# A two-layer RG-LRU / GLA trunk on one core: another opening, GLA values of two heads side by side, three gate projections after the recurrences

## The chip, the core and the metric

The kernel runs on one core of a Trainium2 chip. The core has five engines with queues of their own: TensorE (PE in the profile, with its weight loads as PEld), VectorE (DVE), ScalarE (ACT), GpSimd (POOL) and SyncE (SP), which here issues every DMA. The metric is device time in microseconds of one execution; lower is better. The kernel before was timed three times: 1184.10, 1184.95 and 1185.15 us, median 1184.95 us.

## What is computed

512 positions of 1024 features pass through two layers. Each layer is a token mixer and then a gated ConvFFN, and each of these four sublayers has an RMS norm with adaLN scale and shift ahead and an RMS norm with an adaLN gate behind it. All of it is float32.

```python
def reference(x, c, ...):                       # x (1, 512, 1024), c (1, 1024)
    c_act = jax.nn.silu(c)
    for i in range(2):
        mod = (c_act @ ada_w[i] + ada_b[i])[:, None, :]
        sh_m, sc_m, gt_m, sh_f, sc_f, gt_f = jnp.split(mod, 6, axis=-1)
        h = rmsnorm(x, norm_g[i, 0]) * (1.0 + sc_m) + sh_m
        y = rglru_mixer(h, ...) if i == 0 else gla_mixer(h, ...)
        x = x + gt_m * rmsnorm(y, norm_g[i, 1])
        h = rmsnorm(x, norm_g[i, 2]) * (1.0 + sc_f) + sh_f
        x = x + gt_f * rmsnorm(conv_ffn(h, ...), norm_g[i, 3])
    return x

def rglru_mixer(h, w_in, conv_w, conv_b, wa, ba, wx, bx, lam, w_out):
    gate_br, x_br = jnp.split(h @ w_in, 2, axis=-1)
    x_br = causal_dwconv(x_br, conv_w, conv_b)             # 4 taps
    r   = sigmoid(block_diagonal(x_br, wa) + ba)           # 4 blocks of 256
    i_g = sigmoid(block_diagonal(x_br, wx) + bx)
    a = exp(-8 * r * softplus(-lam)); u = sqrt(1 - a * a) * i_g * x_br
    hs = scan(h_t = a_t * h_{t-1} + u_t)
    return (gelu(gate_br) * hs) @ w_out

def gla_mixer(h, ...):          # q, k: 4 heads of 128; v, r: 4 heads of 256; chunked scan
    q, k, v, r, z = split(h @ w_in); log_alpha = log_sigmoid(z @ w_alpha + b_alpha) / 16
    o = gated_linear_attention(q, k, v, log_alpha)
    return (rmsnorm(o) * silu(r)) @ w_out
```

## The kernel before

Everything is kept transposed: a feature tile is 128 features on the partitions by 512 positions in the columns, so x, h and each product are 8 such tiles. TensorE's products are split: a weight tile is loaded in float32 into a `raw` buffer, ScalarE makes its rounded part (CAST, `w<-raw`), VectorE the rest (TENSOR_TENSOR, `w<-raw,w`), and `mm3` makes three fp32r matmuls of them: high part by high part of h, high by low, low by high. A few small products (`e.mms` on float32 tiles) run as float32 in two passes each, and the trace counts each pass.

The program is not emitted in the order in which it is written. `Sched` records every instruction with its operands and an estimated cost, and `order` makes a list schedule: each engine takes, among its instructions whose operands and buffers its own estimate calls ready, the one with the longest path to the end (TensorE and SyncE: the one that was written first). The engines then run these lists strictly in order, with semaphores between them. Buffers come from pools: 43 general tiles `g`, 8 split weight tiles `w`, 3 `raw`, 2 `araw`, 7 PSUM banks `mm` and one PSUM bank `nr` for the norms' sums.

The stages that the change touches:

- **Opening** (layer 0's first norm and the RG-LRU input products). x comes in 8 loads of 256 KB; ScalarE squares each tile, VectorE adds them up in one sum, `rstd_bcast` sums over the partitions by matmuls with a column of ones (`nr<-const,g`, 128x1), ScalarE scales, GpSimd raises to the power -1/2 (`pow`), VectorE multiplies the identity by the result (`dg`, four TENSOR_SCALAR), and a float32 matmul with ones spreads it over all partitions (`nr<-g,const`). For each input tile k there are then two adaLN columns (`ada_col`: a 512 KB load and one VectorE STT over 1024 columns with a sum, `w<-w,const`), one weight unit `rgx` with the columns of NX = 6 output tiles, and the tile's h: VectorE multiplies by the norm, ScalarE applies scale and shift and casts, VectorE subtracts. The 6 products stay open in 6 PSUM banks over all eight k; the last two (`rgx2`) follow, each in one piece.
- **RG-LRU.** `conv4` takes each input product out of PSUM (one ScalarE instruction, three VectorE STT). `gproj(m)` is a gate projection of 24 matmuls, `gates(b)` the two sigmoid products of block b: float32 on unsplit weights, or fp32r on split ones for the blocks in GFR = (1, 2). `recur` is the recurrence of four tiles, `gmul` the product that goes into `out_proj`. RGG says which gate projections stand ahead of which block: ((), (0,), (1,2,3,4), (5,6,7)), with `gates(3)` last.
- **GLA.** For each head: the diagonal (`diag_start`), the values (`vproj`, 96 matmuls of 256 columns, `mm<-w,g`), two r projections of 24 matmuls of 512 columns, seven levels of the triangle (`level_x` on VectorE and ScalarE, `level_mm`: four float32 matmuls of 64 columns, then a copy_predicated), the part between the chunks (`inter_x`, `inter_mm`), and `attend`.
- **Norms.** All 19 norms go through `rstd_from` with its multiplied identity.

## Time and profile before

| what | value |
|---|---|
| median of three runs | 1184.95 us |
| span of the profiled execution, first to last instruction | 1182.5 us |
| PE busy | 1158.9 us, 98% |
| PEld / DVE / ACT / POOL busy | 1017.0 / 867.3 / 553.6 / 24.4 us |
| first lasting stretch of products on PE | from 23.81 us |
| granted TensorE clock | 0.999 |
| DMA | 157.44 MB, mean 133 GB/s |

The profiled execution's own time is its span, 1182.5 us, 2.45 us under the median. Busy time is a union over an engine's instructions, and a matmul's end is modelled; so what a matmul costs in a stream is read here from the starts of the streams that follow each other, divided by the number of matmuls, and not from the mean duration of one.

### The profile page before, as it was taken

What the parts mean: (1) busy time and instruction counts of PE and PEld (TensorE: products, weight loads), DVE (VectorE), ACT (ScalarE), POOL (GpSimd) and SP (SyncE); (2) the same over time, 40 slices, a digit from 0 to 9 for tenths busy, and PEclk for the clock granted to TensorE, in tenths of its full rate; (3) what the DMA queues carried; (4) which work ended last, traced back from release to release, by engine and by line L of the source; (5) the groups of instructions that cost most, each with busy time, mean ns of one, the idle gap of its engine ahead of it and who ended that gap; (6) DMA issues with size and microseconds to landing.
All of it is one profiled execution on the core that took longest, in us unless ns stands there. A gap on an engine that the chain in (4) does not pass through costs nothing.

```text
span 1182.5 us, 16970 instructions
## 1 busy us (share of the span) xinstructions
PE 1158.9 (98%) x6664; PEld 1017.0 (86%) x6664; DVE 867.3 (73%) x1470; ACT 553.6 (47%) x874; POOL 24.4 (2%) x37
## 2 busy tenths in 40 slices
PE   4999999999999999999999999999999999999998
PEld 3878899988888888899999899999988888888897
DVE  7999999988988956558779767458845556645635
ACT  5688864743333324434478344254643333424421
POOL 1000001000000000000000000000000000000000
PEclk9999999999999999999999999999999999999999
DMA  8956562477787843232412211203243333332202
GB/s 338 312 170 202 200 214 73 160 249 252 249 260 223 261 126 93 88 90 59 144 55 90 72 54 55 72 27 118 72 125 97 100 91 105 90 107 90 72 1 72
DMA packets 45857, 157.44 MB, mean 133 GB/s; under 512 B 4977, under 2 KB 7281, under 8 KB 45778
## 3 DMA queue, kind: packets, MB, share of 16 engines
q1 hardware_dynamic: 45778, 156.36, 41.6%
q8 instruction: 52, 0.85, 0.3%
q14 instruction: 27, 0.22, 0.1%
HBM read 154.25 MB, written 2.10 MB: 132 GB/s over the span
## 4 chain that ended last, share of the span: by engine, by line
PE 90%; DVE 5%; ACT 3%; issue 1%; DMA 1%; SPq 0%; POOL 0%; DVEq 0%; POOLq 0%
PE mm L435 88%; ACT g L411 2%; PE nr L435 1%; DVE g L377 1%; DVE w L364 1%; ACT L411 1%; DVE g L364 1%; ACT w L416 1%; DVE gh L377 1%; DVE g L393 1%; DVE w L377 1%; DMA const<-in_xT_dram 0%; DMA raw<-in_wall_dram 0%; DVE araw L377 0%; SPq L441 0%
## 5 line engine op out<-in xcount | busy, mean ns | idle before, releaser
L435 PE MATMUL mm<-g,w 128*128 128x512 f32 (+1 forms) x5114 | 957.5, 348 | 5.6 <-ACT g L416 2.5
L435 PEld LDWEIGHTS mm<-g,w 128*128 128x128 f32 x5114 | 826.2, 189 | 130.4 <-ACT g L416 4.1
L364 DVE TENSOR_TENSOR w<-raw,w 128x1024 fp32r<-128x1024 f32 (+1 forms) x181 | 217.8, 1205 | 152.4 <-ACT w L416 152.0
L416 ACT CAST w<-raw 128x1024 fp32r<-128x1024 f32 (+1 forms) x181 | 187.2, 1036 | 206.3 <-PE mm L435 202.3
L377 DVE SCALAR_TENSOR_TENSOR g<-mm,const,g 128x511 f32<-128x511 f32 (+3 forms) x208 | 153.3, 745 | 11.2 <-ACT g L411 5.3
L364 DVE TENSOR_TENSOR g<-g,g 128x512 f32<-128x512 f32 (+4 forms) x213 | 126.2, 614 | 37.7 <-ACT g L411 19.4
L411 ACT ACTIVATE g<-mm,const 128x512 f32<-128x512 f32 (+1 forms) x148 | 102.2, 698 | 20.6 <-PE mm L435 20.5
L411 ACT ACTIVATE g<-g 128x512 f32<-128x512 f32 (+1 forms) x132 | 66.7, 540 | 96.2 <-DVE g L377 77.4
L435 PE MATMUL mm<-g,g 128*128 128x256 f32 (+4 forms) x748 | 102.1, 293 | 0.0
L435 PEld LDWEIGHTS mm<-g,g 128*128 128x128 f32 (+1 forms) x748 | 94.8, 191 | 3.8
L416 ACT CAST g<-g 128x512 fp32r<-128x512 f32 (+1 forms) x74 | 45.4, 614 | 107.7 <-DVE g L364 105.0
L377 DVE SCALAR_TENSOR_TENSOR araw<-araw,const 128x1024 f32<-128x1024 f32 x72 | 87.1, 1220 | 9.2 <-DMA araw<-in_adaT_dram 9.0
L364 DVE TENSOR_TENSOR g<-g,mm 128x512 f32<-128x512 f32 (+1 forms) x80 | 44.9, 577 | 44.5 <-PE mm L435 44.2
L364 DVE TENSOR_TENSOR gh<-gh,gh 128x256 f32<-128x256 f32 x97 | 40.4, 420 | 22.2 <-ACT gh L411 20.6
L435 PE MATMUL mm<-w,g 128*128 128x256 f32 x384 | 49.6, 288 | 0.0
L435 PEld LDWEIGHTS mm<-w,g 128*128 128x128 f32 x384 | 46.9, 192 | 1.4 <-issue 1.4
L368 POOL TENSOR_TENSOR sm<-sm,const 128x2 f32<-128x2 f32 (+1 forms) x19 | 19.4, 1022 | 1025.7 <-DVE sm L388 1018.5
L411 ACT ACTIVATE gh<-g 128x256 f32<-128x256 f32 x32 | 13.1, 416 | 51.3 <-DVE g L364 51.3
L411 ACT ACTIVATE g<-gh,const 128x256 fp32r<-128x256 f32 x48 | 21.9, 503 | 26.4 <-DVE gh L377 26.2
L411 ACT ACT_TABLE_LOAD x24 | 30.8, 1283 | 1.1 <-PEq L1242 0.7
L377 DVE SCALAR_TENSOR_TENSOR w<-w,const 128x1024 f32<-128x1024 f32 x24 | 28.8, 1217 | 0.0
L411 ACT ACTIVATE gh<-const 128x256 f32<-128x256 f32 x48 | 18.9, 414 | 20.1 <-DVE const L364 20.0
(66 smaller groups left out, 465.6 us busy)
## 6 DMA issues: line engine op xcount, KB each, us to landing
raw<-in_wall_dram SPq DMA_DIRECT2D x186, 512.0 KB, 3.7
araw<-in_adaT_dram SPq DMA_DIRECT2D x72, 512.0 KB, 4.5
w<-in_adaT_dram SPq DMA_DIRECT2D x24, 512.0 KB, 5.8
raw<-in_wall_dram SPq DMA_DIRECT2D x8, 384.0 KB, 6.7
const<-in_xT_dram SPq DMA_DIRECT2D x8, 256.0 KB, 4.1
out_dram<-const SPq DMA_DIRECT2D x8, 256.0 KB, 2.1
araw<-in_masks_dram SPq DMA_DIRECT2D x1, 512.0 KB, 5.2
const<-in_par_dram SPq DMA_DIRECT2D x1, 291.0 KB, 3.6
```

The lines of the kernel that those rows point to most:

```text
L364: self.s.add(eng, dur, lambda: e.tensor_tensor(out.ap(), a.ap(), b.ap(), op=op), [a, b], [out])
L368: lambda: self.nc.gpsimd.tensor_tensor(out.ap(), a.ap(), b.ap(), op=ALU.pow), [a, b], [out])
L377: return self.nc.vector.scalar_tensor_tensor(out.ap(), a.ap(), f(sc), b.ap(), op0=op0, op1=op1, **kw)
L393: lambda: self.nc.vector.tensor_tensor_scan(out.ap(), a.ap(), b.ap(), 0.0, op0=ALU.mult, op1=ALU.add),
L411: return self.nc.scalar.activation(out.ap(), a.ap(), func, **kw)
L416: self.s.add("act", (0.095 if self._sb(a) else 0.052) + out.n * 0.8325e-3, lambda: self.nc.scalar.copy(out.ap(), a.ap()), [a], [out])
L435: r.append(self.nc.tensor.matmul(g[0].ap(), g[1].ap(), g[2].ap(), start=g[3], stop=g[4], **kw))
```

## The change

- **x and parameters.** Four loads of 512 KB, each of two tiles of x; the parameter columns in two loads, the first 160 columns behind x and the other 422 later, at k = 4 as it is written.
- **First norm.** The squares go into four sums (tiles 0 to 3, 4 and 5, 6, 7), each of which the partition sum takes by itself in one PSUM group; two float32 matmuls of 512 columns on x are written between (the first ahead of the first sum). ScalarE's table for silu is loaded by a first instruction on one column.
- **rstd_from, all norms.** The identity is no longer multiplied on VectorE; the matmul takes the rstd column, repeated 128 times by a stride of zero, as its weights, and the identity as its moving operand: per 128 positions one float32 matmul of 128 columns.
- **Input products.** NX = 8: all eight are open at once, seven in `mm` and the eighth in the `nr` bank; `rgx` units have 1024 columns and the `rgx2` units are gone. h is made by `h_tile`, as in the other sublayers: STT on VectorE, Identity with shift on ScalarE, STT on VectorE.
- **RGG** = ((0,), (1,), (2, 3), (4,), (5, 6, 7)); the last group is written behind `gates(3)` and `recur`. GFR = (1,), so `gates(2)` becomes float32.
- **GLA.** `vproj(pair, t)` makes the values of two heads for 128 positions in 24 matmuls of 512 columns. `GLA_CHUNKS` lists the 8 value and 8 r products, `GLA_ENDS` = (6, 9, 14, 16) says how many are written by the end of each head, and a head's diagonal, levels and inter part are written in between them in equal parts. `level_mm` and its copy work on the first 64 (level of 64) or 96 rows (level of 32).
- **Sched.** Other cost figures (`mms`, `scan`, `pow`, loads), 0.12 us between dependent VectorE instructions, and a look-ahead: VectorE does not start an instruction when a more urgent one becomes ready while it would run.

```diff
-RGG = ((), (0,), (1,2,3,4), (5,6,7))
-NX = 6
+RGG = ((0,), (1,), (2, 3), (4,), (5, 6, 7))
+NX = 8
+GLA_CHUNKS = ([("v", t) for t in range(4)] + [("r", 0), ("r", 1), ("r", 2), ("r", 3), ("v", 4), ("v", 5),
+              ("v", 6), ("v", 7), ("r", 4), ("r", 5), ("r", 6), ("r", 7)])
+GLA_ENDS = (6, 9, 14, 16)
...
-GFR = (1, 2)
+GFR = (1,)
...
+                if e in LOOK and any(r < t + o.dur - 0.05 and ops[i].prio < o.prio - (r - t) - 1.5 and can_alloc(ops[i])
+                                     for r, i in wait[e]):
+                    heapq.heappush(cand[e], (o.prio, o.idx))
+                    continue
...
-        dg = s.buf("gh", F32, 256) if nt <= 2 else gt()
-        for t in range(nt):
-            e.ts(dg[t * P:(t + 1) * P], ident[:], rp[t:t + 1], None, ALU.mult)
-        e.mms([(nr[0:nt * P], ones[:], dg[0:nt * P], True, True)])
+        e.mms([(nr[t * P:(t + 1) * P], rp[t:t + 1].map(lambda a: a.to_broadcast([P, P]), P), ident[:], True, True)
+               for t in range(nt)])
...
+    for j, a in enumerate(sums0):
+        for _ in range(WARM[j]):
+            e.mms([(idle[:], ones[:], x[0], True, True)])
+        e.mms([(nr0[t:t + 1], a[t * P:(t + 1) * P], ones[0:1], j == 0 and t == 0, j == len(sums0) - 1, True)
+               for t in range(NT)])
+    rb0 = rstd_from(nr0, NT, D, True)
...
-    xps = [mmtile() for _ in range(NX)]
+    rs0 = gt()
+    e.acopy(rs0[:], rb0[:])
+    xps = [mmtile() if m < MMB else s.buf("nr") for m in range(NX)]
...
-            e.act(hf[sl], xn[sl], AF.Identity, bias=mcol(0, 0, k), scale=mcol(0, 1, k))
-            e.acopy(hh[sl], hf[sl])
-            e.tt(hl[sl], hf[sl], hh[sl].f32(), ALU.subtract)
+            h_tile(h, k, sl, (rs0 if k else rb0)[sl], sl.stop - sl.start, 0, 0)
...
+    for m in RGG[4]:
+        gproj(m)
...
+        rows = P - hb
+        rows = rows if rows <= 96 else P
+        e.mms([(ps[t * n:(t + 1) * n].rows(rows), xt[t * P:t * P + rows], part3(xt[tsl(t)], 2 * hb, hb, 2 * hb),
+                True, True) for t in range(NT)])
...
+        small = [start] + [lambda lv=lv: level(lv) for lv in range(len(LEVELS))] + [inter]
+        chunks = GLA_CHUNKS[done:GLA_ENDS[hd]]
+        done = GLA_ENDS[hd]
+        given = 0
+        for n, (what, i) in enumerate(chunks):
+            vproj(i // NT, i % NT) if what == "v" else rproj(i)
+            upto = len(small) * (n + 1) // len(chunks)
+            for f in small[given:upto]:
+                f()
+            given = upto
+        attend(hd, ats[0], axs[0])
```

What the schedule makes of it, at three places. The first is ScalarE's list in the opening, between the last squares of x (`g<-const`, 128x512) and the first h; `sm<-nr` is the scaling of the norm's sums. Before:

```order
L411 ACTIVATE g_170<-const_86 128x512
L411 ACTIVATE const_186<-const_176,const_134,const_89 128x1
L411 ACTIVATE sm_193<-nr_178,const_91 128x4
L416 CAST w_197<-raw_109 128x768
L411 ACTIVATE const_186<-const_176,const_89 128x1
L411 ACTIVATE const_186<-const_176,const_134,const_89 128x1
L416 CAST w_220<-raw_115 128x768
L411 ACTIVATE const_186<-const_176,const_89 128x1
L411 ACTIVATE g_226<-g_222,const_186 128x256
L416 CAST g_230<-g_226 128x256
```

Now:

```order
L431 ACTIVATE g_159<-const_86 128x512
L431 ACTIVATE const_175<-const_169,const_157,const_95 128x1
L436 CAST w_179<-raw_105 128x1024
L431 ACTIVATE sm_181<-nr_149,const_90 128x4
L431 ACTIVATE const_175<-const_169,const_95 128x1
L436 CAST w_195<-raw_111 128x1024
L431 ACTIVATE g_201<-gh_197,const_175 128x256
L431 ACTIVATE g_201<-gh_199,const_175 128x256
L436 COPY g_206<-nr_149 128x512
```

The scaling of the sums now stands behind the first weight unit's CAST, where it stood ahead of it; and the first h takes one ScalarE instruction where it took two.

The second place is TensorE's list at the end of `gates(3)` (`mm<-g,raw`). Before, `out_proj` follows (`mm_1212`, 128x256, the first rows by tiles 0 to 2 of its operand):

```order
L435 MATMUL mm_1194<-g_664,raw_836 128x512
L435 MATMUL mm_1202<-g_623,raw_836 128x512
L435 MATMUL mm_1202<-g_664,raw_836 128x512
L435 MATMUL mm_1212<-g_964,w_1068 128x256
L435 MATMUL mm_1212<-g_989,w_1068 128x256
L435 MATMUL mm_1212<-g_964,w_1068 128x256
L435 MATMUL mm_1212<-g_974,w_1068 128x256
```

Now:

```order
L455 MATMUL mm_1002<-g_643,raw_722 128x512
L455 MATMUL mm_1010<-g_635,raw_722 128x512
L455 MATMUL mm_1010<-g_643,raw_722 128x512
L455 MATMUL mm_1024<-g_201,w_819 128x512
L455 MATMUL mm_1024<-g_204,w_819 128x512
L455 MATMUL mm_1024<-g_201,w_819 128x512
L455 MATMUL mm_1024<-g_241,w_819 128x512
```

Here `mm_1024` is the gate projection of tile 5, and tiles 6 and 7 follow it; 72 matmuls of 512 columns now stand between `gates(3)` and `out_proj`.

The third place is TensorE's list in GLA's first head. Before, all seven levels (`128x64`) stand in one row behind the values and both r projections (`mm_5923` is the second):

```order
L435 MATMUL mm_5923<-g_5152,w_5478 128x512
L435 MATMUL mm_5973<-g_5717 128x64 x4
L435 MATMUL mm_5980<-g_5725 128x64 x4
L435 MATMUL mm_5988<-g_5734 128x64 x4
L435 MATMUL mm_5995<-g_5759 128x64 x4
L435 MATMUL mm_6005<-g_5781 128x64 x4
```

Now (`mm_5716` and `mm_5787` are values of two heads, 128 positions each):

```order
L455 MATMUL mm_5716<-w_5428,g_5102 128x512
L455 MATMUL mm_5771<-g_5667 128x64 x4
L455 MATMUL mm_5779<-g_5674 128x64 x4
L455 MATMUL mm_5787<-w_5197,g_4951 128x512
L455 MATMUL mm_5787<-w_5197,g_4963 128x512
```

The first two levels now come after three of the four value products, and the others between the products that follow.

## Rows read from the trace of the kernel before

**Rows 1.** The page: span, and busy tenths in 40 slices of 29.6 us.
```profile
span 1182.5 us, 16970 instructions
...
PE   4999999999999999999999999999999999999998
...
DVE  7999999988988956558779767458845556645635
```
**Rows 2.** Waits of PE: who for whom, us in total, times, longest.
```profile
PE nr L435 <- DVE g L364: 7.0, 1, 7.0
PE nr L435 <- DVE g L388: 3.2, 1, 3.2
```
**Rows 3.** Windows: us, busy us (instructions) of each engine, PEclk, DMA share, GB/s.
```profile
0.00:5.00 5.00, 2.55 (x3) 1.16 (x4) 0.00 (x0) 2.10 (x3) 0.52 (x8) 1.00 0.54 170
5.00:10.00 5.00, 1.20 (x2) 0.00 (x0) 3.29 (x11) 4.35 (x7) 1.64 (x1) 1.00 0.96 325
10.00:15.00 5.00, 1.75 (x8) 1.75 (x8) 4.41 (x14) 2.28 (x4) 0.00 (x0) 1.00 1.02 415
...
570.00:580.00 10.00, 9.01 (x72) 8.40 (x71) 8.90 (x19) 3.86 (x8) 2.22 (x6) 1.00 0.58 159
```
**Rows 4.** Timeline of the opening: start, us, engine, what, count [idle before <-releaser].
```profile
10.25 1.94 ACT L411 ACTIVATE g<-const 128x512 f32<-128x512 f32 x3 [0.87 <-DMA const<-in_xT_dram]
...
13.25 1.87 PE L435 MATMUL nr<-const,g 128*128 128x1 f32 x8 [7.05 <-DVE g L364]
...
15.37 0.82 ACT L416 CAST w<-raw 128x768 fp32r<-128x768 f32 x1
15.55 1.56 POOL L368 TENSOR_TENSOR sm<-sm,const 128x4 f32<-128x4 f32 x1 [7.25 <-ACT sm L411]
...
17.27 0.86 DVE L388 TENSOR_SCALAR g<-const,sm 128x128 f32<-128x128 f32 x4
...
18.28 2.05 PE L435 MATMUL nr<-g,const 128*128 128x512 f32 x2 [3.16 <-DVE g L388]
...
20.06 1.22 DVE L377 SCALAR_TENSOR_TENSOR w<-w,const 128x1024 f32<-128x1024 f32 x1
...
21.72 0.60 ACT L411 ACTIVATE g<-g,const 128x256 f32<-128x256 f32 x1
...
23.81 8.46 PE L435 MATMUL mm<-g,w 128*128 128x256 f32 x47 [0.42 <-DVE g L364]
```
**Rows 5.** Timeline of PE in the RG-LRU stage.
```profile
68.82 7.03 PE L435 MATMUL mm<-g,raw 128*128 128x512 f32 x16
...
136.57 13.75 PE L435 MATMUL mm<-g,w 128*128 128x256 f32 x110
151.12 16.58 PE L435 MATMUL mm<-g,w 128*128 128x256 f32 x136 [0.81 <-DVE w L364]
```
**Rows 6.** Timeline of PE in GLA's first head.
```profile
608.96 11.76 PE L435 MATMUL mm<-w,g 128*128 128x256 f32 x96
620.55 11.07 PE L435 MATMUL mm<-g,w 128*128 128x512 f32 x48
631.46 6.36 PE L435 MATMUL mm<-g 128*128 128x64 f32 x56
637.66 2.45 PE L435 MATMUL mm<-g,g 128*128 128x128 f32 x20
```
**Rows 7.** PE's weight loads by shape: count, busy us, mean ns, idle before.
```profile
L435 PEld LDWEIGHTS mm<-g 128*128 128x128 f32 x224 | 25.6, 192 | 0.3
...
L435 PEld LDWEIGHTS mm<-g,w 128*32 128x32 f32 x32 | 3.5, 109 | 1.7 <-ACT g L411 0.9 <-DVE g L377 0.5
```
**Rows 8.** Timeline of VectorE in the tail, the last norm.
```profile
1173.67 0.48 DVE L388 TENSOR_SCALAR gh<-const,sm 128x128 f32<-128x128 f32 x2 [0.88 <-POOL sm L368]
...
1174.94 3.22 DVE L377 SCALAR_TENSOR_TENSOR gh<-g,const,nr 128x256 f32<-128x256 f32 x8 [0.79 <-PE nr L435]
```
**Rows 9.** Timeline of VectorE where conv4 takes input products out of PSUM.
```profile
57.98 4.28 DVE L377 SCALAR_TENSOR_TENSOR g<-mm,const,g 128x511 f32<-128x511 f32 x6
```

More of the change, by code (lines that the diff above doesn't have):

```diff
@@ L153, in buf, with add @@
         return b
-    def add(self, eng, dur, fn, reads, writes, xfer=0.0, table=None, after=()):
+    def add(self, eng, dur, fn, reads, writes, xfer=0.0, table=None, after=(), late=0.0):
         o = Op()
+        o.late = late
         o.eng, o.dur, o.fn, o.idx, o.xfer = eng, dur, fn, len(self.ops), xfer
@@ L366, in pow @@
     def pow(self, out, a, b):
-        self.s.add("pool", 0.3 + 0.165 * out.n,
+        self.s.add("pool", 0.6 + 0.165 * out.n,
                    lambda: self.nc.gpsimd.tensor_tensor(out.ap(), a.ap(), b.ap(), op=ALU.pow), [a, b], [out])
@@ L438, in mms, with load, accum @@
         return self.s.add("pe", dur, fn, reads, writes, after=after)
-    def load(self, out, src, nbytes, after=()):
+    def load(self, out, src, nbytes, after=(), late=0.0):
         self.s.add("sp", 0.05, lambda: self.nc.sync.dma_start(out.ap(), src), [], [out], xfer=nbytes / 360e3,
-                   after=after)
+                   after=after, late=late)
+    def accum(self, out, src, nbytes):
+        self.s.add("pool", 1.2, lambda: self.nc.gpsimd.dma_start(out.ap(), src, accum_op=ALU.add), [out], [out],
+                   xfer=nbytes / 180e3)
     def store(self, dst, v, nbytes):
@@ L449, in memset @@
                    after=after)
+BYLOAD = lambda what, *i: False
+SQ_GROUPS = ((0, 1, 2, 3), (4, 5), (6,), (7,))
+WARM = (1, 1, 0, 0)
 KSPLIT = 2
@@ L625, in ada @@
         raw = s.buf(ring, F32, 2 * D if ring == "w" else D)[0:D]
-        e.load(raw, adaT[layer, jt], P * D * 4)
+        e.load(raw, adaT[layer, jt], P * D * 4, late=LATE[1] if layer or jt >= 2 * KD else 0.0)
         e.stt(raw, raw, 1.0, cact[:], ALU.mult, ALU.mult, accum=mraw[layer][jt:jt + 1])
@@ L962, in trunk @@
             recur(range(2 * b - 2, 2 * b + 2))
+    for m in RGG[4]:
+        gproj(m)
     for m in range(KD):
```

175 lines of the change are left out of this document (95 added, 80 removed).

## Prediction

> **What bounds the kernel now.** I read the slices first [rows 1]: PE is at 9 from the second slice to the last but one, so what counts is when its stream of products starts, how much work is in it, the few places where it waits, and the tail. VectorE is at 8 or 9 in the first twelve slices too, so whatever starts PE earlier must also leave VectorE time. The waits come next [rows 2]: the two largest, 7.0 and 3.2 us, are both for the first norm, and the timeline of the opening [rows 4] shows the chain behind them. The last squares of x start at 10.25, three sums on VectorE follow, PE sums over partitions from 13.25 (1.87 us), GpSimd's power takes 1.56 us from 15.55, the multiplied identity 0.86 us from 17.27, PE spreads it from 18.28 (2.05 us), an adaLN column holds VectorE from 20.06 for 1.22 us, two ScalarE steps per half follow (the first 0.60 us), and products run without a break from 23.81. From there the only long waits are 0.81 us at 151.12, for the end of the recurrence [rows 5], and 0.99 us around 570 to 580, for GLA's first h [rows 3]. So 23.8 us of opening are about 2% of the span, and most of that is not PE's work.
>
> **The opening, a gain of 5.1 us.** I rebuild the chain with the rows' durations. DMA first: by the rates of the windows [rows 3], 170, 325 and 415 GB/s for 5 us each, 0.85 MB have come by 5 us, 2.47 by 10 and 4.55 by 15. Ahead of the end of the first weight tile stand x (2.10 MB), the first parameters and the identity (0.15), one adaLN column and the tile (0.52 each): 3.29 MB, so 12.0 us, and I add 0.3 for landing (2.46 MB had been asked for up to the last x, and ScalarE got it at 10.25). The squares are not late then: one sum instead of three stands behind them. But in ScalarE's new list the scaling of the sums comes behind the first CAST, 0.82 us for 768 columns and so 1.1 for 1024: 12.3 + 1.1 + 0.3 gives 13.7. The power follows, 1.56, and 0.1 for each hand-over: 15.4. Then PE spreads it with eight passes of 128 columns, without VectorE. Eight small passes took 1.87 us here [rows 4] and 0.9 at the pace of GLA's levels (56 passes in the 6.20 us from 631.46 to 637.66, 0.111 each [rows 6]), although the granted clock reads 1.00 in both; so 16.4 to 17.4. Then three steps of half a tile: VectorE 0.40 (eight in 3.22 us [rows 8]), ScalarE 0.60, VectorE 0.40, with their hand-overs 1.7 us: products run without a break from 18.1 to 19.1, and I take 18.7. The second adaLN column that this h needs ends its 0.52 MB at 13.5, and its 1.22 us on VectorE stand behind the weight tile's subtraction; it is done by 16 and hidden. The bounds: if the tiles land 2 us later than their share of bytes, 20.7; if the power runs beside a CAST that comes earlier, 17. The gain is 3 to 7 us.
>
> Will PE then run on? A tile k now has 24 matmuls of 0.227 us (48 in the 10.91 us from 620.55 to 631.46 [rows 6]), 5.5 us, where it had 18, 4.1 us. VectorE has per tile two adaLN columns and a subtraction of 1024 columns (1.2 each) and two of 512 columns (about 0.65 each): 4.9 us. That fits under 5.5 and would not have fitted under 4.1; DMA brings the 1.57 MB of a tile in 3.8 us at 415 GB/s. The total of the input products doesn't change: 192 matmuls' worth before and after.
>
> **PE's work, a gain of 3.2 us.** The values of GLA: 96 matmuls of 256 columns take the 11.59 us from 608.96 to 620.55, 0.1207 each [rows 6]. 384 of these are 46.4 us; 192 of 512 columns at 0.227 are 43.6. That is 2.7 us less, on PE's path throughout. `gates(2)` goes the other way: 24 matmuls at 0.227 are 5.5 us, and 16 float32 passes at 0.43 (16 in 6.5 to 7.0 us [rows 5]) are 6.7: 1.2 us more; VectorE gets back a weight split and two splits of inputs. The level of 64 loads weights of 64 columns instead of 128, 32 passes in all. No row has such a load; 128 columns take 192 ns and 32 take 109 [rows 7], so between them about 136 ns, 55 ns less. A pass costs 0.111 us, more than its 64 columns need by the pace of 512, so the load sets it, and I take 32 times 0.055, 1.7 us; the bounds are 0, if something else sets it, and 2.6, if the level of 32 with its 96 rows gains too. The norms' 128-column matmuls have as many columns as those that they replace: nothing.
>
> The Trainium skill ("TensorE: Matmul & The Clock Gate", section "Back-to-back issue gap") gives a lone stream one column per cycle and 2.5 ns per matmul: 109 ns for 256 columns, 216 for 512. By that, as an estimate, the joined values would gain only 0.5 us. The rows show 120.7 and 227, 11 ns more for either, and so I stay with 2.7.
>
> **Waits, a gain of 0.3 us.** The 0.81 us at 151.12 goes: three gate projections, 72 matmuls or 16.3 us, stand between `gates(3)` and `out_proj` and cover the recurrence's last steps. What is late next is `out_proj`'s own first evacuation, which needs eight adaLN columns. Each norm loses two VectorE steps (0.48 us [rows 8]); of the 0.99 us before GLA's first h I take half. New is the end of the opening: all eight banks are full, and the next product needs one that `conv4` has emptied: three STT of 0.71 us (six in 4.28 [rows 9]) after a ScalarE step, 2.1 us of VectorE per bank. The first bank's product ends 4.8 us ahead of the last one's, which about covers it; I take 1.0 us, bounds 0 and 5. Behind PE's waiting matmul are the sigmoid products, and ScalarE and the recurrence wait for these. GLA's levels between the projections I cost at nothing: their VectorE steps stand ahead of the same amount of PE work as before, and the projections hide them; uncovered they would be about 2 us per level.
>
> **The tail, a gain of 0.5 us.** The last norm's two VectorE steps, 0.48 us [rows 8], are on the path to the end.
>
> **The sum.** 5.1 + 3.2 + 0.3 + 0.5 = 9.1 us off the span of 1182.5: 1173.4. The median was 2.45 above the span, so 1175.9, rounded to 1176.
>
> **The rivals.** *The opening stays long* (0.14): the small tiles' DMAs come in several at a time, the first weight tile lands late, and PE starts at about 21.5 and waits again for tiles 2 and 3, as two adaLN columns for later are now loaded among them. Against it stands that VectorE has no small constants in its way there any more. 4.5 us of the 9.1 go: 1180.5.
>
> *The head start is paid back at the first FFN* (0.10): VectorE's list now has 7 of the later adaLN columns ahead of the last input of `out_proj`, where the trace had 17; ten at 1.2 us come later, beside the norms of `out_proj`. If VectorE, at 9 in those slices [rows 1], sets the first FFN's start, the 5.1 us go back: 1181. Against it: its list up to there is shorter by three weight splits.
>
> *Joining gains nothing per column* (0.05): PE's cost per column is the same in a wide matmul, and the 0.0135 us that a 256-column one has over half a wide one were waits of the first head's stream; then 2.2 of the 2.7 us stay away: 1178. This is what the Trainium skill's section named above amounts to.
>
> *Banks hold PE, slower* (0.08): after the eight open products one bank comes free per 2.1 us at best, VectorE's weight splits and the 20 small steps for the decay constants stand between, and one product plus the first two blocks need nine banks. Eight times 2.1 is 17 us; all of it on the path, instead of 1.0, gives 1176 + 16 = 1192. It decides from 10 us of waits on. Against it: before, the same STTs ran beside PE, and its stream shows no such wait from 23.81 to 151.
>
> *It doesn't do what it says*: the lists show each move made, so I give it no chance of its own.
>
> **How the numbers follow.** The forecast has 0.63, and its bounds (opening 2 us either way, levels 1.7, banks 4 one way) give 1171 to 1180. The likeliest rivals lie at 1178 to 1181, so 1170.5 to 1183 leaves out the banks and some of the edges, less than 2 in 10. A measurement here tells 0.2% (2.4 us) from no change. Faster than 1182.6: the forecast and the three milder rivals, less what of them reaches beyond, 0.86; slower than 1187.3: 0.08; between: 0.06.
>
> **What would show it.** The stream of products should start between 17 and 21 us in PE's timeline and run with 24 matmuls per 5.5 us; the values should come 24 to 5.5 us; the wait ahead of `out_proj` should be gone; PE should wait under 2 us between the last input product and `gates(1)`; and the step of VectorE between power and spreading should be missing from all norms. I am wrong if PE's waits after its start add up to more than 5 us, or if the first product starts after 22.

## The result: 3.2 us slower

The changed kernel takes 1188.06 us (median of 8 runs, 1186.24 to 1190.18), the kernel before 1184.82: a ratio of 1.0028 (1.0018 to 1.0038). The forecast was 1176.0. The profiled execution has a span of 1186.1 and a time of 1188.26.

| place on PE (us) | before | after | difference |
|---|---|---|---|
| products run without a break from | 23.81 | 19.61 | -4.2 |
| the eight input products done | 68.82 | 65.45 | -3.4 |
| `out_proj` runs without a break from | 136.57 | 138.72 | +2.2 |
| first FFN, its run of 114 products | 218.72 | 225.11 | +6.4 |
| GLA's first product of 96 rows | 601.76 | 607.43 | +5.7 |
| first norm of GLA's `out_proj` | 781.11 | 783.51 | +2.4 |
| last norm's first sums | 1170.87 | 1174.24 | +3.4 |
| span | 1182.5 | 1186.1 | +3.6 |

So the opening gained its 4.2 us, GLA its 3.3, and the stretch between 20 and 225 us gave back 10.6. In some executions of a kernel with the new opening, PE's sums take 3.8 us, in others 6.8 (short and long sums below), and the latter are some 2 to 4 us longer; medians mix the two, and where it matters below, like is compared with like (executions without a trace are told apart by their time and mean granted clock, see the end).

### The profile page after: what moved, and what is told of

Same layout as the page of the kernel before. It is cut to its first block, busy times and chain, and to the rows that moved or that the text cites. A ratio compares the mean times of both kernels' runs of the same rounds, so it can differ in the third digit from the quotient of the medians.

```text
span 1186.1 us, 16663 instructions
## 1 busy us (share of the span) xinstructions
PE 1166.5 (98%) x6556; PEld 1013.5 (85%) x6556; DVE 857.3 (72%) x1414; ACT 546.1 (46%) x861; POOL 26.2 (2%) x37
## 4 chain that ended last, share of the span: by engine, by line
PE 90%; DVE 4%; ACT 2%; issue 2%; DMA 1%; POOL 1%; SPq 0%; DVEq 0%; POOLq 0%; ACTq 0%
PE mm L455 88%; PE nr L455 2%; DVE gh L384 1%; ACT g L431 1%; POOL sm L388 1%; DMA w<-in_adaT_dram 1%; ACT L431 1%; DVE g L397 0%; DVE g L384 0%; DVE gh L397 0%; DMA raw<-in_wall_dram 0%; DVE const L384 0%; DVE w L397 0%; DVE w L384 0%; SPq L461 0%
## 5 line engine op out<-in xcount | busy, mean ns | idle before, releaser
L455 PE MATMUL mm<-g,w 128*128 128x512 f32 (+2 forms) x5069 | 951.3, 348 | 6.1 <-DVE w L384 1.9
L455 PEld LDWEIGHTS mm<-g,w 128*128 128x128 f32 (+1 forms) x5069 | 817.5, 190 | 126.8 <-DVE g L397 2.2
L436 ACT CAST w<-raw 128x1024 fp32r<-128x1024 f32 x178 | 185.8, 1046 | 213.9 <-PE mm L455 204.3
L384 DVE TENSOR_TENSOR w<-raw,w 128x1024 fp32r<-128x1024 f32 x178 | 215.6, 1216 | 86.1 <-ACT w L436 85.4
L397 DVE SCALAR_TENSOR_TENSOR g<-mm,const,g 128x510 f32<-128x510 f32 (+3 forms) x205 | 151.1, 746 | 99.3 <-ACT g L431 88.8
L384 DVE TENSOR_TENSOR g<-g,g 128x512 f32<-128x512 f32 (+2 forms) x199 | 117.6, 612 | 34.5 <-ACT g L431 27.1
L436 ACT CAST g<-g 128x512 fp32r<-128x512 f32 (+1 forms) x63 | 38.9, 620 | 108.3 <-DVE g L384 106.3
L455 PE MATMUL mm<-w,g 128*128 128x512 f32 x192 | 46.2, 394 | 0.0
L455 PEld LDWEIGHTS mm<-w,g 128*128 128x128 f32 x192 | 35.4, 188 | 7.0
L436 ACT COPY g<-mm 128x512 f32<-128x512 f32 (+1 forms) x36 | 19.7, 560 | 23.9 <-PE mm L455 23.9
```

The costliest lines, as they stand in the source:

```text
L384: self.s.add(eng, dur, lambda: e.tensor_tensor(out.ap(), a.ap(), b.ap(), op=op), [a, b], [out])
L397: return self.nc.vector.scalar_tensor_tensor(out.ap(), a.ap(), f(sc), b.ap(), op0=op0, op1=op1, **kw)
L436: self.s.add("act", (0.095 if self._sb(a) else 0.052) + out.n * 0.8325e-3, lambda: self.nc.scalar.copy(out.ap(), a.ap()), [a], [out])
L455: r.append(self.nc.tensor.matmul(g[0].ap(), g[1].ap(), g[2].ap(), start=g[3], stop=g[4], **kw))
```

## The profile after

The page, to be read beside [rows 1]:

```profile
span 1186.1 us, 16663 instructions
...
PE   7999899999999999999999999999999999999998
...
DVE  5998989987777888777859666758745556645644
...
PEclk8999999999999999999999999999999999999999
```

PE's first slice is fuller, but there is a new 8 in the fifth, and VectorE has 5, 8, 8 in the first, fourth and sixth slice where it had 7, 9, 9. The opening (timeline, columns as in [rows 4]):

```profile
9.59 3.77 PE L455 MATMUL nr<-const,g 128*128 128x1 f32 x32
...
13.08 1.03 ACT L436 CAST w<-raw 128x1024 fp32r<-128x1024 f32 x1
14.01 0.25 ACT L431 ACTIVATE sm<-nr,const 128x4 f32<-128x4 f32 x1
...
14.41 1.82 POOL L388 TENSOR_TENSOR sm<-sm,const 128x4 f32<-128x4 f32 x1 [13.36 <-ACT sm L431]
16.29 2.07 PE L455 MATMUL nr<-const,sm 128*128 128x128 f32 x8 [2.93 <-POOL sm L388]
...
18.48 0.87 DVE L397 SCALAR_TENSOR_TENSOR gh<-const,const,nr 128x256 f32<-128x256 f32 x2 [0.82 <-PE nr L455]
...
19.61 4.66 PE L455 MATMUL mm<-g,w 128*128 128x256 f32 x21 [1.25 <-ACT g L431]
```

The waits of PE from there to 260 us, 6.6 us in all:

```profile
PE mm L455 <- DVE w L384: 1.9, 1, 1.9
PE mm L455 <- ACT g L431: 1.6, 2, 1.3
PE mm L455 <- DVE g L397: 1.4, 1, 1.4
PE nr L455 <- DVE gh L384: 1.2, 1, 1.2
PE mm L455 <- ACT w L436: 1.1, 1, 1.1
```

(1.3 of the second row is the wait at 19.61 itself.) The first large ones stand where `out_proj` begins: timelines of PE, ScalarE and VectorE.

```profile
136.35 0.51 PE L455 MATMUL mm<-g,w 128*128 128x256 f32 x2 [1.14 <-ACT w L436]
138.72 2.69 PE L455 MATMUL mm<-g,w 128*128 128x256 f32 x14 [1.86 <-DVE w L384]
...
135.25 1.05 ACT L436 CAST w<-raw 128x1024 fp32r<-128x1024 f32 x1 [1.17 <-PE mm L455]
...
135.16 1.21 DVE L397 SCALAR_TENSOR_TENSOR w<-w,const 128x1024 f32<-128x1024 f32 x1
136.30 0.08 DVE L397 DVE_READ_ACCUMULATOR w<-w,const 128x1 f32 x1
136.30 1.21 DVE L397 SCALAR_TENSOR_TENSOR araw<-araw,const 128x1024 f32<-128x1024 f32 x1
...
137.45 1.21 DVE L384 TENSOR_TENSOR w<-raw,w 128x1024 fp32r<-128x1024 f32 x1
```

`out_proj`'s first weight unit is rounded at 135.25, when a gate projection gives up a weight slot, and split at 137.45, behind two adaLN columns; before, VectorE had split three units between 128.3 and 136.4. After this wait the granted clock falls, to 0.50 (1.2 GHz) between 140 and 142 us (windows of the changed kernel, columns as in [rows 3]): 74 matmuls in the second window instead of 86, about 1.5 us.

```profile
130.00:140.00 10.00, 7.01 (x35) 5.56 (x34) 10.00 (x14) 5.05 (x8) 0.00 (x0) 0.98 0.31 89
140.00:150.00 10.00, 10.00 (x74) 10.00 (x74) 9.56 (x17) 3.49 (x6) 0.00 (x0) 0.85 0.81 270
```

And one account will decide the case: what PE and VectorE do up to the FFN's run of 114. First the kernel before, then the changed one (third pair of numbers: VectorE).

```profile
0.00:20.00 20.00, 7.34 (x14) 3.44 (x14) 12.53 (x38) 10.00 (x16) 3.72 (x10) 1.00 0.89 330
20.00:218.72 198.72, 194.14 (x1137) 168.67 (x1137) 191.81 (x345) 137.62 (x228) 4.36 (x4) 1.00 0.59 200
```
```profile
0.00:20.00 20.00, 13.48 (x49) 8.36 (x49) 8.87 (x16) 10.60 (x20) 2.34 (x9) 0.83 0.90 337
20.00:225.11 205.11, 198.33 (x1143) 169.55 (x1142) 189.59 (x347) 129.43 (x213) 7.21 (x5) 0.98 0.55 190
```

Columns after the length: PE, PEld, VectorE, ScalarE, GpSimd. Before, from 20 us on, PE had 4.6 us and VectorE 6.9 us to spare. After, VectorE does 3.7 us less in the first 20 us, nearly as much behind them, and is idle for 15.5. The 3.7 us are not the decay constants alone: the new opening also has three additions of x's squares less (some 2.4 us) and no multiplied identity (0.86 us [rows 4]), and other steps have come forward.

## The experiments

All times are medians; the ratio to the kernel before and its interval stand in brackets.

### Which part of the change costs

**GLA alone** (`x_b_gla`): before, with the new functions of the GLA stage.

```
-        vproj(hd)            # 256 columns a head
+        vproj(pair, t)       # 512 columns, two heads; projections and levels in turn
```

> The kernel before with the new GLA stage alone (values of two heads in 512 columns, projections and levels interleaved, the levels' shorter weight loads); everything up to the end of the first FFN is as before. In the changed kernel the stretch from the first z product to the first norm of GLA's out_proj took 176.08 us instead of 179.35. Theory: that is PE work, so all of it reaches the end, 1184.8 - 3.3 = 1181.5, range 1180.5 to 1182.5. Rival: the second FFN's start is set by adaLN columns and norms on VectorE and gives it back, 1183.5 to 1185.

1181.53 (0.9972, 0.9961 to 0.9982): 3.4 us, as in the changed kernel's trace. This part works and reaches the end.

**The norms' spreading besides** (`x_b_gla_rstd`).

```
-        e.ts(dg[t * P:(t + 1) * P], ident[:], rp[t:t + 1], None, ALU.mult)
+        e.mms([(nr[...], rp[t:t + 1] broadcast, ident[:], True, True) for t in range(nt)])
```

> The kernel before with the new GLA stage and, besides, the norms' spreading by PE with the power as broadcast weights, without VectorE's two to four multiplications of the identity; opening, planner and grouping as before. With GLA alone it was 1181.53. As forecast for the norms: the tail's 0.5 us and up to 0.5 us at GLA's first h, 1180.5. Rival, from the tail of the changed kernel (1.27 us from the power's end to VectorE's next step, 1.30 before): four weight loads per two token tiles take the time that the two VectorE steps gave back, 1181.0 to 1182; and the shorter opening chain (0.86 us less on VectorE) alone may show, 1180.7.

1180.43 (0.9958, 0.9943 to 0.9973): 1.1 us. The tail from the last sums to VectorE's next step is 3.61 us instead of 4.08, and the 0.99 us of waits before GLA's first h are gone. In the changed kernel the tail gained nothing, and PE's timeline shows why; this run first, then the changed kernel.

```profile
1169.68 1.54 PE L440 MATMUL mm<-const,const 128*128 128x256 f32 x6
1171.06 0.61 PE L440 MATMUL nr<-const,sm 128*128 128x128 f32 x4
```
```profile
1175.83 1.97 PE L455 MATMUL mm<-const,const 128*128 128x256 f32 x8
1177.64 0.61 PE L455 MATMUL nr<-const,sm 128*128 128x128 f32 x4
```

There the planner put eight idle identity products ahead of the spreading, not six, and they end 0.6 us behind the power.

**The opening alone, the order alone**, each on top of the last one.

```
x_open_only:  + new opening      RGG, GFR, prices, look-ahead of before
x_order_only: + RGG = ((0,), (1,), (2, 3), (4,), (5, 6, 7)); GFR = (1,); LOOK = ("dve",); new prices
              opening of before
```

> The kernel before with the new GLA stage, the new spreading of the norms and the new opening (eight open products, no constants ahead on VectorE); planner, grouping of the gate projections and the second float32 block as before. GLA and norms alone gave 1180.43 with products from 22.45. Theory P (the new planner and grouping are what pays the head start back): the opening's gain comes through, 1177 to 1179. Theory V (up to the first FFN VectorE has as much to do as there is time; PE's head start is waited away again): 1180 to 1183, with new waits of 2 to 4 us before out_proj or the first h. In the executions in which the sums take 6.83 us, 2 to 3 us more.

1184.64 (1.0003, 0.9992 to 1.0014).

> The kernel before with the new GLA stage and norms and with the new planner (prices, look-ahead, late adaLN loads), the new grouping of the gate projections and the third float32 block; the opening as before. GLA and norms alone gave 1180.43, all parts together 1188.06. Theory P: most of the 7.6 us between them are here, 1184 to 1188, with the waits ahead of out_proj and the first FFN as in the changed kernel. Theory V: without the head start there is nothing to pay back, 1180.5 to 1182.5 (1.4 us for the float32 block).

1183.08 (0.9980, 0.9971 to 0.9990). So the changes nearly add up: from 1180.43, the opening costs 4.2 us, the order 2.7 (1.0 of it the float32 block), both together 7.6. Theory P falls for its larger half: with planner and grouping of before the opening doesn't bring its head start to the end, it loses time. PE waits 3.3 us between the input tiles (2.5 for VectorE, 0.8 for ScalarE), and VectorE is busy for 68.8 of the 70 us from 60 to 130, as it was before: there is no room there in which the lost time could be made up. The account from 20 us up to the run of 114 products, first for GLA and norms alone, then, with the longest of these waits, for the opening besides:

```profile
20.00:219.85 199.85, 195.28 (x1145) 169.16 (x1146) 193.55 (x339) 137.90 (x228) 3.82 (x4) 1.00 0.61 206
```
```profile
42.80 6.45 PE L455 MATMUL mm<-g,w 128*128 128x512 f32 x20 [1.93 <-DVE g L397]
...
20.00:223.27 203.27, 196.97 (x1150) 170.10 (x1151) 193.80 (x353) 130.02 (x215) 6.53 (x5) 0.98 0.58 196
```

Behind 20 us VectorE has as much to do as without the new opening (193.8 us, 193.55 there), but it is idle for 9.5 us in between instead of 6.3, and the run of 114 begins 3.4 us later.

### Attempts on the order

```
x_nolook:       -LOOK = ("dve",)                     +LOOK = ()
x_oldrgg:       -RGG = ((0,), (1,), (2, 3), (4,), (5, 6, 7))
                +RGG = ((), (0,), (1, 2, 3, 4), (5, 6, 7), ())
x_oldsched:     LOOK = () and all prices, LATE and xlat of before
x_gfr12:        -GFR = (1,)                          +GFR = (1, 2)
x_early:        -o.prio = -o.tail                    +o.prio = -o.tail - 40 for 24 adaLN columns
x_early_oldrgg: x_early and x_oldrgg
x_byload:       -BYLOAD = lambda what, *i: False     +... what == "rgo"
```

> The changed kernel without the planner's look-ahead (LOOK empty), all else as changed. The changed kernel starts its lasting stream of products 4.2 us earlier than before (19.61 against 23.81), yet begins out_proj 2.15 us later (138.72 against 136.57) and the first FFN's stream 6.4 us later. Theory A (the planner holds VectorE idle for dearer steps to come, VectorE stood idle for about 5 us between 80 and 135 us, so adaLN columns, and with them the weights that share their slots, come late): out_proj starts by 136.5, the two waits of 1.14 and 1.86 us before it go, and the time falls by 3 to 6 us, to 1182 to 1185. Theory B (the last three gate projections are what brings out_proj's weights late): out_proj still starts at 138 or later and the time stays within 1.5 us of 1188. Theory C (VectorE is the bound up to the first FFN, the head start is paid back whatever the order): out_proj moves, the first FFN does not, time 1187 to 1189.

1197.17 (1.0101, 1.0084 to 1.0118). All three theories missed it: the four projections that run from 77.36 in the changed kernel run from 83.89. Some 3 us of that are the long sums of the traced execution (products from 22.62); 2.0 are waits of PE between the input tiles, for VectorE and ScalarE, which the changed kernel doesn't have. Behind them come waits of 2.3, 2.0 and 1.8 us at 144.9, 175.6 and 202.6; what makes the rest of the loss isn't followed up.

> The changed kernel with the gate projections grouped as before (none, 0, 1 to 4, 5 to 7 ahead of the four blocks of gates, none behind), all else as changed. Theory B (three projections behind the last gates take the weight slots and the ScalarE time that out_proj's first weights need): the waits of 1.14 and 1.86 us before out_proj go, the 0.81 us for the recurrence comes back, and the time falls by 2 to 4 us, to 1184 to 1186. Theory A (the look-ahead defers adaLN columns): out_proj's weights are late all the same, 1187 to 1190, for the wait on the recurrence comes on top. Theory C: out_proj moves by up to 2 us, the first FFN does not, 1187 to 1189.

1187.72 (1.0023, 1.0013 to 1.0032). `out_proj` now starts at 134.18 without a wait, as theory B said; but most of the time comes back at the first FFN, whose run of 114 begins at 223.50, 1.6 us earlier than in the changed kernel (like with like the times say the same: 1186.3 to 1187.2 against 1186.2 to 1188.7 with short sums, medians 1.5 us apart). PE, VectorE and ScalarE there:

```profile
187.42 1.95 PE L455 MATMUL mm<-g,w 128*128 128x256 f32 x6 [4.14 <-ACT g L431]
...
185.40 1.22 DVE L397 SCALAR_TENSOR_TENSOR araw<-araw,const 128x1024 f32<-128x1024 f32 x1
186.54 0.08 DVE L397 DVE_READ_ACCUMULATOR araw<-araw,const 128x1 f32 x1
186.66 0.17 DVE L384 TENSOR_TENSOR const<-const,const 128x8 f32<-128x8 f32 x1
...
186.86 1.31 ACT L431 ACTIVATE g<-gh,const 128x256 fp32r<-128x256 f32 x3 [2.79 <-DVE const L384]
```

The last adaLN column of the shift ends at 186.6, and h follows at once: the rival of the prediction, in the trace.

> The changed kernel with the planner of before: no look-ahead, and the prices of before for steps that follow each other on VectorE, scans, powers, matmuls and late adaLN columns. Theory A in its wider form (the new prices and the look-ahead together order VectorE worse): 1180 to 1184, with the first FFN's stream of 512 columns starting by 237 (changed kernel 241.38, before 234.99) and at least 2 us of the VectorE idle time between 80 and 135 us gone. Theory A in its narrow form (look-ahead alone): as without the look-ahead, within 1 us. Theories B and C: within 1.5 us of 1188.

1188.12 (1.0020, 1.0010 to 1.0029): no gain by the median, but 6 of these 10 executions had long sums, against 1 of 8 of the changed kernel. Like with like it is some 2 us faster: 1185.1 to 1185.9 against 1186.2 to 1188.7 with short sums, 1188.1 to 1189.8 against 1190.18 with long ones. Theory A's 1180 to 1184 is missed all the same; the planner is a small part of the loss.

> The changed kernel with the third block of gates again multiplied in parts (GFR = 1 and 2) instead of in float32: on PE 24 matmuls at 0.227 us in place of 16 passes at 0.43, 1.4 us less by the traces (6.46 to 6.86 against 5.45), on VectorE one weight split and two splits of inputs more, about 2.5 us. Rival D: 1.4 us faster, 1186.7. Theory C: VectorE is what counts, so nothing is gained or up to 2.5 us lost, 1188 to 1190.5.

1190.97 (1.0042, 1.0028 to 1.0056). The median is 2.9 us above the changed kernel's, but two of the six executions, the traced one with short sums among them, took 1187.1 and 1187.8, as in the changed kernel; the other four took 1190.8 to 1191.9. In the traced one `out_proj` runs from 136.69, 2.0 us earlier, and PE then waits 4.44 us for the first h:

```profile
190.98 1.31 PE L455 MATMUL mm<-g,w 128*128 128x256 f32 x3 [4.44 <-ACT g L431]
...
225.01 16.43 PE L455 MATMUL mm<-g,g 128*128 128x256 f32 x114
```

The run of 114 begins where it did (225.11). PE has 1.0 us less to do and nothing comes of it: theory D falls. Whether VectorE's 2.5 us more cost anything on top isn't shown.

> The changed kernel with the 24 adaLN columns of layer 0's parts 2, 4 and 3 moved up in the planner's priorities by 40 us, so that VectorE takes most of them between 25 and 120 us (the list has only six behind the first product of out_proj, where the changed kernel's has eighteen); no work is added or left out. Theory G (not the amount of VectorE's work but its order: the columns put off hold weight slots that out_proj's first units wait for, and stand ahead of the norms of the first FFN): the 3.0 us of waits before out_proj, the 1.5 us of low clock after them and most of the 3.6 us of waits at the first FFN go, 1188 - 7 = 1181, range 1179 to 1184. Rival H (the three gate projections behind the last gates fill the slots by themselves): out_proj's waits stay, 1186 to 1188.

1186.13 (1.0009, 1.0000 to 1.0018), 1.9 us less than the changed kernel (2.2 with short sums alone). The waits at the first FFN go but for 0.56 us, but PE now waits 4.09 us ahead of `out_proj` for the recurrence, and VectorE is busy throughout:

```profile
144.34 5.91 PE L456 MATMUL mm<-g,w 128*128 128x256 f32 x33 [4.09 <-DVE g L385]
...
140.00:150.00 10.00, 5.91 (x36) 5.56 (x35) 10.00 (x15) 5.15 (x8) 0.00 (x0) 0.83 0.00 0
```

> As the run with early adaLN columns, and with the gate projections grouped as before. With the old grouping and late columns, out_proj started at 134.18 without a wait, but PE waited 4.14 us for the first h of the FFN, right behind the last shift column, and lost about 1.5 us to the lower clock after it. Theory G: that wait goes, 1187.7 - 5.5 = 1182, range 1180 to 1184, and no better than the early columns alone by more than 2 us. Rival H: this one is 3 us or more faster than the early columns with the new grouping.

1193.03 (1.0064, 1.0049 to 1.0079): early columns and early projections leave VectorE no time for `conv4`, and PE waits 8.3 us between 69 and 92. Early columns win 2 us of the 7 that theory G gave them with the new grouping, and lose with the old one: that only their order is at fault falls.

> The changed kernel with the low parts of out_proj's eight weight units made by ScalarE (minus the rounded part) and an adding DMA from GpSimd's queue, in place of eight VectorE subtractions of 1.22 us. Theory C: 9.8 us less on VectorE just where it is late, so 4 to 7 us faster, 1181 to 1184, if the adding DMAs are no slower than 4 us each. Rival E (the weights of out_proj are late for their slots and their loads, not for VectorE): the longer way through a second DMA makes out_proj later still, 1189 to 1193.

1200.80 (1.0132, 1.0116 to 1.0147), for another reason: the first unit of `out_proj` arrives through its second DMA only at 144.5 (PE waits 3.61 us for ScalarE, then 3.01 for the DMA). Rival E; it says nothing on VectorE.

### VectorE's amount of work

Both kernels with some 22 us of VectorE's work left out (24 adaLN columns take 0.28 us each instead of 1.22, and 7 of 8 parts of their sums are missing), first in the unchanged order, then laid out anew:

```
-        e.stt(raw, raw, 1.0, cact[:], ALU.mult, ALU.mult, accum=acc)
+        the same on raw[0:128], cact[0:128] for layer 0, parts 2, 4, 3; planned at 1.14 us (short) or 0.2 us (replanned)
```

> The changed kernel in the same order, instruction for instruction; only the 24 adaLN columns of layer 0's gate, scale and shift ahead of the first FFN (parts 2, 4 and 3) are multiplied and summed over 128 of their 1024 elements, with the same loads and slots. That is about 1 us less on VectorE for each, 24 us in all, and it leaves out 7 of 8 parts of these sums. Theory C (VectorE's list, with these columns in it, sets the start of out_proj and of the first FFN's h, so PE's head start cannot come through): the 3.0 us of waits ahead of out_proj, the 1.5 us of low clock behind them and the 3.5 us of waits at the first FFN go, 1188 - 8 = 1180, range 1178 to 1182. Rival D (PE's own work, three float32 blocks of gates instead of two and the cold start, eats the head start): at most the waits of 1.9 us, 1186 to 1188.

> The kernel before with the same 24 adaLN columns summed over 128 of 1024 elements, order and loads untouched; 7 of 8 parts of these sums are left out. Theory C: before, VectorE reached the first h only just in time (PE waited 0.66 us there and 0.81 us at 151.12), so little is to be had: 1184.9 - 1.5 = 1183.4, range 1182.3 to 1184. Then the changed kernel gains several times as much by the same edit, and the difference of the two shortened kernels is what the change is worth to PE: 1183.4 - 1180 = 3.4 us in favour of the changed one. Rival D: before gains as much as the changed one, and the changed one stays 2 to 4 us behind.

1186.83 (1.0013, 1.0002 to 1.0024) and 1184.97 (0.9997, 0.9988 to 1.0007): far less than theory C said (like with like, with short sums, 1184.1 to 1185.5 against 1186.2 to 1188.7, some 3 us). In a list in fixed order the columns' place is what holds others up: PE still waits 1.77 us for the same late CAST.

> The changed kernel with the 24 adaLN columns summed over 128 of 1024 elements (7 of 8 parts left out) and, unlike in the first run of this, priced so in the planner, which can use the 24 us that VectorE wins. With the order unchanged that gave 1186.83. Theory V: with VectorE relieved and its list laid out for it, out_proj starts without a wait at 134 to 136 and the first h is there in time: 1179 to 1182. Theory P: the look-ahead and the grouping still bring out_proj's weights late: 1185 to 1188.

> The kernel before with the 24 adaLN columns summed over 128 of 1024 elements (7 of 8 parts left out) and priced so in its planner. With the order unchanged that gave 1184.97, no gain. Theory V: before, VectorE's list just fitted, so only the 1.7 us of waits between 136 and 218 us can go: 1183 to 1184. Theory P says the same of it; what is told apart is whether the changed kernel gains several times more by the same edit.

1180.14 (0.9956, 0.9939 to 0.9972) and 1184.44 (0.9996, 0.9986 to 1.0005). The changed kernel gains 7.9 us, the one before 0.7. So the changed kernel's start of the first FFN hangs on VectorE's work together with its layout; before, VectorE's work didn't set it: 22 us less of it gained at most 0.7.

### The decay constants put back

The new opening loads the constants' parameters late and computes them behind the input products. Put back into the opening:

```
-    e.load(par[0:NPAR0], par_d[:, 0:NPAR0], P * NPAR0 * 4)
+    e.load(par[:], par_d, P * NPAR * 4)
+    lam = pcol("rg_lambda", 0, 8)  ... the whole block, ahead of the sums
-        if k == 4:  e.load(par[NPAR0:NPAR], ...)
```

> The run with the new opening on the planner and grouping of before, with one thing put back: all parameters are loaded at once in the opening and the decay constants' 19 small VectorE steps (3.3 us by the rows of before) stand ahead of the first weight tile, in VectorE's idle time, instead of behind the input products. Theory V (from 20 us on VectorE has 190 to 194 us to do before the first FFN runs free, so what counts is what it gets done before 20 us: 12.5 us before, 8.6 with the new opening): 3 us come back, 1184.6 - 3 = 1181.6, range 1180.5 to 1183. Rival: the constants hold up the first weight tile or the power on GpSimd and the products start later for it, 1184 to 1187.

1183.76 (0.9983, 0.9973 to 0.9994). Executions with long sums were more frequent here (6 of 8, against 3 of 10); like with like it is 3.3 us with short sums and 3.8 with long ones, by their means: 1180.8 and 1181.2 against 1183.3 to 1184.7 with short sums, 1183.1 to 1184.9 against 1187.5 to 1188.6 with long ones. Theory V said 3. But the opening is then only no loss: 1181.0 with short sums stands beside 1180.43 for GLA and norms alone. The constants account for most of the 4.2 us. Why nothing is left of the head start itself (products from 20.32 with the opening alone, from 22.45 with GLA and norms) stays open; the rows show a VectorE that is busy almost throughout.

> The changed kernel with the parameters loaded at once and the decay constants computed ahead of the input products where the planner finds room (11 of the small steps stand ahead of the first weight tile, the others between the tiles). Theory V: 1.5 to 3 us come back, 1185 to 1186.5. Rival (the planner's new order is what counts): within 1 us of 1188 or worse.

1180.15 (0.9962, 0.9949 to 0.9975): 7.9 us less than the changed kernel, and within the noise of GLA with norms alone (1180.43): even here the new opening and order gain nothing. PE, ScalarE and VectorE ahead of `out_proj`, and the account up to the run of 114 products:

```profile
138.58 1.69 PE L455 MATMUL mm<-g,w 128*128 128x256 f32 x12 [0.80 <-DVE w L384]
...
129.94 1.04 ACT L436 CAST w<-raw 128x1024 fp32r<-128x1024 f32 x1
...
132.54 1.21 DVE L384 TENSOR_TENSOR w<-raw,w 128x1024 fp32r<-128x1024 f32 x1
...
0.00:20.00 20.00, 14.28 (x52) 9.08 (x53) 10.37 (x28) 10.75 (x20) 3.17 (x10) 0.83 0.91 353
20.00:217.96 197.96, 195.16 (x1141) 167.54 (x1141) 186.95 (x334) 130.42 (x214) 4.36 (x4) 0.99 0.57 196
```

With 12 of the block's small steps in the opening (19 of its 28 stood there before), two more adaLN columns are done by 60 us (18 instead of 16), the first unit of `out_proj` is rounded 5.3 us earlier, and PE's waits up to 260 us shrink from 6.6 to 2.7; the clock doesn't fall. Of the 7.1 us by which the run of 114 comes earlier, 0.8 are the start, 3.9 the waits and 2.3 shorter work on PE, of which 1.5 is the low clock behind the wait at 138.72. That is more than the 1.5 us of VectorE's work that moved; the list changed in other places with it, and what of the gain is the work and what is a luckier list isn't told apart. The short kernel, laid out anew, gained the same 7.9 us by leaving out some 22 us of VectorE's work. So another place in VectorE's list can give as much as less work; that its amount counts apart from that isn't shown.

### The clock in the opening

```
+    for _ in range(6):  e.mms([(idle[0:P], ones[:], ones[:], True, True)])     # ahead of c
+    for _ in range(2):  e.mms([(idle[:], ones[:], x[0], True, True)])          # ahead of the spreading
```

> The changed kernel in its order with idle float32 matmuls added on PE: six of 128 columns on the ones before the first use of c, and two of 512 columns between the sums over partitions and the spreading. In the traces so far the 32 passes of the sums took 3.8 us in some executions and 6.83 in others, the products started at 19.0 to 19.6 or at 21.3 to 21.7 accordingly, and in both the first 24 products ran at half pace. Theory W (the opening's PE steps depend on a clock that is not raised in every execution): sums at 3.8 us in each execution, spreading in 0.9 instead of 2.07, first 24 products in 2.9 instead of 4.7, so 2 to 3 us off the good executions and the spread of the times down from 4 us to under 1.5: 1185, range 1184 to 1186. Rival: the clock falls all the same while PE waits for VectorE and ScalarE, and the two idle matmuls only delay the spreading where the sums are slow: 1188 to 1190.

1190.71 (1.0039, 1.0027 to 1.0050): theory W falls, and no execution was faster than 1187.77. PE was at full pace sooner (the first eight passes of the sums in 1.05 us), but the other 24 then took 5.11, at a granted clock of 0.50.

## Why the prediction was wrong, step by step

**The opening** was nearly right on PE: products from 19.61, 0.9 later than taken and within the outer bound of 20.7, with the CAST at 13.08 where I had 12.3, and the power at 1.82 instead of 1.56. (With long sums they start later: at 21.37 in the trace of `x_after_short`, beyond that bound.) The tiles then came every 5.45 us without a wait.

**The step that failed is to carry these 5.1 us to the end.** I held it in favour of the opening that "VectorE has no small constants in its way there any more", and cost their move at nothing. But of the first twelve slices it is the first, at 7 in [rows 1] and not at the "8 or 9" that I read, in which VectorE had most room. It did 12.5 us of work in its first 20 us before and 8.9 after; the constants, some 3 us, went into a stretch in which VectorE had 6.9 us to spare in 198.7. Alone, the opening costs 4.2 us, and with the constants back 3.3 to 3.8 of them return. That makes up for the loss; the 5.1 us of gain stay away even so. Of the 12 us between forecast and result some 9 are the opening's (5.1 forecast, 4.2 lost), 1 is GLA's, and the rest the order's and what the two do to each other. The rival "The head start is paid back at the first FFN" named the place, but bounded its price by the head start (1181). The price has no such bound: PE's waits were 6.6 us, and behind the long one came 1.5 us at a lower clock.

**`gates(2)`** measured 1.0 us (6.46 to 5.45), forecast 1.2 (by its own 0.43 a pass, 16 passes are 6.9 us and not 6.7, and the term 1.4). But that it is on PE's path doesn't make it time: `x_gfr12`, which takes it back, begins the run of 114 no earlier.

**Waits.** The 0.81 us at 151.12 went, but I had read it wrongly. Its row [rows 5] names not the recurrence but a step on a weight tile, VectorE's split, which stood behind the recurrence's last steps and ended at 151.07:

```profile
149.85 1.22 DVE L364 TENSOR_TENSOR w<-raw,w 128x1024 fp32r<-128x1024 f32 x1
```

Gate projections don't cover that, and PE's largest wait is now for such a split again, 1.86 us at 138.72. What was late was not `out_proj`'s first evacuation but its first weight unit: three gate projections and the adaLN columns held the slots until 135. This is the new wait of a moved step, in the queue that I had not looked at. The banks did not hold PE: no wait from 19.61 to 135.

**GLA** gained 3.3 us of the 4.4 forecast. The values are right: 24 products of 512 columns in 5.45 us, 0.227 each.

```profile
613.81 5.60 PE L455 MATMUL mm<-w,g 128*128 128x512 f32 x24
...
646.46 0.81 PE L455 MATMUL mm<-g 128*96 128x64 f32 x8
```

Two matmuls of 256 columns at 0.1207 less one of these are 0.0144 us, 2.8 us over 192. (The rival on joining names 0.0135 us for one such matmul over half a wide one; by the rows it is 0.0072.) What the Trainium skill's section "Back-to-back issue gap" ("TensorE: Matmul & The Clock Gate") would give for them as an estimate, 0.5 us from its figures for matmuls by themselves, doesn't agree with these rows. The levels' term was mis-sized, on both sides: the level of 64 goes at 0.075 us a pass and the level of 32, with 96 rows, at 0.079 (8 passes in 0.63 us), against 0.111 in [rows 6], so some 1.1 us for 32 passes of each, where I had 1.7 and "if the level of 32 with its 96 rows gains too" only in the bounds; but a projection that stands behind a level now takes 5.54 to 5.66 us instead of 5.45, which makes 1.5 to 2 us if it holds for all 16.

**The tail's** 0.5 us are there when the norms are changed alone, and covered in the changed kernel by two identity products more ahead of the spreading. I had not looked where the planner put these.

My own test, "wrong if PE's waits after its start add up to more than 5 us", spoke: 6.6.

## What to carry over

When two engines are each over 96% busy in a stretch, a head start for one isn't time won: here PE's came to nothing with VectorE's small steps left in the opening, and to a loss with them moved out. Compare both engines' work from the point at which the head start begins to the next point where they meet, and then look at what stands in which place in the busier one's list. A step that leaves an idle opening is not gone: price it where it lands. And an edit that helps one part (here GLA and the norms, 4.5 us) should be measured apart from one that moves work, or the sum hides both.

## What the runs showed of the hardware

The same opening ran in two ways. PE's 32 passes of the sums took 3.77 us in one execution and 6.83 in another of the same instructions, and the products began at 19.61 and at 21.37:

```profile
9.65 6.83 PE L455 MATMUL nr<-const,g 128*128 128x1 f32 x32
18.05 2.07 PE L455 MATMUL nr<-const,sm 128*128 128x128 f32 x8 [1.58 <-POOL sm L388]
```

The granted clock reads 1.00 in every window of the slow case up to 26 us, although the passes go at little more than half the pace; in the quick case it reads 1.00 up to 12 us, 0.82 from 12 to 14, where the sums end, and 0.50 (1.2 GHz) from 14 to 22. The first 21 products of the changed kernel take 0.214 us each there (19.61 to 24.11), the 21 from 24.47 on 0.120. With idle products ahead (`x_warm`) it read 0.70 from 10 to 12 and 0.50 from 12 to 26, with PE busy for most of that time. So a reading of 1.00 early in a program does not say that PE ran at 2.4 GHz; the pace of known passes does. In the profiled executions the mean clock of the span goes with it (0.991 to 0.995 with quick sums, 0.997 to 1.000 with slow ones, but for `x_byload`, which has other long waits, and `x_warm`, whose sums were in part quick); in other executions the two groups are taken from the times and clocks of one kernel, so `x_gfr12`, with 0.988 to 0.997, can't be sorted by it. What decides between the two no row shows. After PE's waits of 3.0, 4.1 and 4.1 us ahead of `out_proj` and the first FFN (the changed kernel, `x_oldrgg`, `x_early`) the lowest window of 10 us read 0.85, 0.65 and 0.83.
